# One load of a fused transformer block, its DRAM side written as eight groups of sixteen rows

## Chip, cores, metric

The kernel runs on one core of a Trainium2 chip. The metric is device time in microseconds of one execution. Three runs of the kernel before gave 1547.07 to 1547.58, median 1547.14.

## What is computed

The reference is one transformer block on 256 tokens of width 2048: a gated spatial unit and a forgetting attention side by side, then a mixture of 32 experts in four groups. Only the experts matter here; a token goes to two of them.

```python
def expert_block(args):
    xi, e = args
    return (jax.nn.silu(xi @ w_g[e]) * (xi @ w_u[e])) @ w_d[e]

yb = lax.map(expert_block, (xb, blk_e)).reshape(P, D)
y = jnp.zeros((T + 1, D), jnp.float32).at[buf_tok].add(yb.astype(jnp.float32) * buf_gate[:, None])[:T]
```

`w_g` and `w_u` are 2048 x 512 for each expert, `w_d` ("down") is 512 x 2048, all float32: 12 MB an expert, and every expert's weights are read.

## The kernel before

The first part (projections, attention, output projection, router) takes some 640 us. Then a loop goes over the 32 experts. For each, `gather` collects its tokens (up to 32), `hidden` multiplies them by gate and up, `times_up` combines the two, and `down` multiplies by the down matrix.

The weights come through SBUF homes of 16 KB a partition (`hT0`, `hT1`, `so0`, `so1`, `rb`, two ring tiles, `third`, and `ex` with `bm` as two halves). Each expert has six chunks `t = 6 e + ...` of 2 MB: two of gate, two of up, two of down. `order` lists the chunks, `free` the homes that are empty, and `load` pairs the next chunk with the next home and issues its DMA from SP. `used_up` gives a home back after PE has read it and calls `load` again. So SP's queue holds one stream of weight loads, and each of them waits for its home and for an earlier landing.

The last two experts (30 and 31) are treated apart. Their down matrices are cut into column blocks, listed in `BLOCKS`: four of 512 columns for expert 30; three of 512 and two of 256 for expert 31. A block of n columns is 128 rows (partitions) of 4 n floats, so 8 KB a row for 512 columns, 1 MB in all. `layout` on the host lays these blocks side by side in `we_l`, 32 KB a partition and expert, and `load` fetches each with a DMA of its own (line 568). `block(e, c0, n)` names the place in SBUF. For expert 31 the chunk that holds the columns from 1024 on goes to the home `hT0`: blocks (31, 1024) with 512 columns, (31, 1536) and (31, 1792) with 256 each. These are the last three loads of the program; in the profile they are `hT<-in_we_l`.

Behind the expert loop stands a loop over `todo`, the nine blocks in order. For each, `columns` (line 927) multiplies on PE into `y_ps`; ACT (line 1075) copies the result into `fine` (also under the name `hT` in the profile), and DVE (line 1076) writes the rounding rest beside it. Then, for the block before this one, `add_columns` spreads the rows to the tokens with four matmuls (line 936), and DVE adds them, times the gate, to the accumulator (line 941, `mT` in the profile). PE's order is fixed by `keep`: `y_ps` of block i, then the four matmuls of block i - 1. When a block of expert 31 has been added, SP stores two pieces of 128 tokens (line 1082).

Of the kernel before, what the change touches and what calls it, by code (L numbers as in the profile page):

```python
# [26 lines left out]
NE = NG * EPG  # L27
# [4 lines left out]

BLOCKS = {NE - 2: ((0, 512), (512, 512), (1024, 512), (1536, 512)),
          NE - 1: ((0, 512), (512, 512), (1024, 512), (1536, 256), (1792, 256))}
QW = 2048
HW = 2 * QW
CUTS = (0, 2, 4, 6, 8, 12, 16)
# [8 lines left out]
def hybrid_block(ctx: ExitStack, tc: tile.TileContext, a, out, dbg=None):  # L46
    nc = tc.nc
# [62 lines left out]
    def early(pool, name, dt=F32R):  # L110
        return pool.tile([P, QW], dt, tag=name, name=name)

    home = {}

    def wide_tile(pool, name, dt=F32R):
        t = pool.tile([P, HW], dt, tag=name, name=name)
        home[id(t)] = pool, name
        return t

    def halves(pool, name):  # L120

        both = [wide_tile(pool, f"{name}{k}") for k in range(2)]
        return [[t[:, i * QW:(i + 1) * QW].rearrange("p (a b) -> p a b", a=8) for i in range(2)] for t in both]

# [426 lines left out]
    def load(n=1):  # L551


        while n and free and order:
            n -= 1
            t = order.popleft()
            slot[t] = free.popleft()
            w = slot[t][0]
            e, m, c = t // 6, t // 2 % 3, t % 2
            src = a[names[m]][e * P:(e + 1) * P]  # L560
            if m < 2 or e not in BLOCKS:
                n0 = HW // len(w)
                for i, wi in enumerate(w):
                    nc.sync.dma_start(wi, src[:, c * HW + i * n0:c * HW + (i + 1) * n0])
            else:
                for c0, n0 in BLOCKS[e]:
                    if c0 // 1024 == c:
                        nc.sync.dma_start(block(e, c0, n0), a["we_l"][e - NE + 2][:, 4 * c0:4 * (c0 + n0)])

    def quarter(t, c):  # L570

        w = slot[t][0]
        return w[c] if len(w) == 2 else w[0][:, c * QW:(c + 1) * QW]

    def block(e, c0, n0):

        o = c0 % 512
        return quarter(6 * e + 4 + c0 // 1024, c0 // 512 % 2)[:, 4 * o:4 * (o + n0)]

    def room(tiles, keep=True):  # L580

        for t in tiles:
            free.append((t if isinstance(t, tuple) else (t,), keep))

    def used_up(t):

        if slot[t][1]:
            free.append(slot[t])
            load()

    mT = None
    for n in range(4):
# [18 lines left out]
        if n == 3:  # L611
            room([wide_tile(ra, nm, F32) for nm in ("hT0", "hT1")])
            load(AHEADS[0])
# [3 lines left out]
        if n == 3:  # L617
            room([wide_tile(ra, "so0", F32)])
            load(AHEADS[1])
# [67 lines left out]
    lent = wide_tile(mp, "mT0", F32)  # L687
    y, acc0 = lent[:, :QW], lent[:, QW:]
    room([lent], False)
# [28 lines left out]
    lent = wide_tile(mp, "mT1", F32)  # L718
    acc = [acc0, lent[:, QW:]]
    room([lent], False)  # L720
# [348 lines left out]
    for i in range(len(todo) + 1):  # L1069
        nxt = None  # L1070
        if i < len(todo):
            e, c0, n = todo[i]
# [4 lines left out]
        if i:  # L1077
            e, c0, n = todo[i - 1]
# [8 lines left out]
def layout(inputs):  # L1087
    import numpy as np

    g = {k: np.asarray(v) for k, v in inputs.items()}  # L1090
    c = np.ascontiguousarray

    def ktile(w):

        return w.reshape(-1, P, w.shape[1]).transpose(1, 0, 2)

    def chunks(w):
        return [ktile(w[:, i:i + 512]) for i in range(0, w.shape[1], 512)]

    def rows4(w):  # L1100

        return c(w.reshape(NE, 4, P, 4 * DE).transpose(0, 2, 1, 3).reshape(NE * P, 16 * DE))

    def columns(e, i, n):

        return g["w_expert_down"][0][e].reshape(4, P, D)[:, :, i:i + n].transpose(1, 0, 2).reshape(P, 4 * n)

    x = g["x"][0]
    w = g["w_in"][0]
    order = [w[:, SW:2 * SW], w[:, 0:SW], w[:, 2 * SW:5 * SW]]  # L1110
    g0 = 5 * SW + NH
    for n in range(4):
        order += [w[:, g0 + n * 512:g0 + (n + 1) * 512], w[:, g0 + D + n * 512:g0 + D + (n + 1) * 512]]
    wp = np.concatenate([g["w_proj_sgu"][0], g["w_proj_fox"][0]], axis=0)
    return {
        "x": c(x.reshape(NT, P, D).transpose(1, 0, 2)),
        "xT": c(ktile(c(x.T))),
        "g1T": c(g["norm1_g"][0].reshape(KT, P).T),
        "g2T": c(g["norm2_g"][0].reshape(KT, P).T),
        "g2p": c(g["norm2_g"][0].reshape(4, P, 4).transpose(1, 2, 0)),  # L1120
        "w_in": c(np.stack([t for o in order for t in chunks(o)])),
        "wf": c(ktile(w[:, 5 * SW:5 * SW + NH])),
        "b_forget": c(g["b_forget"][0]),
        "b_gate": c(g["b_gate"][0]),
        "ln_g": c(g["sgu_ln_g"][0]),
        "ln_b": c(g["sgu_ln_b"][0]),
        "wsT": c(g["w_spatial"][0].transpose(2, 0, 1)),
        "bsT": c(g["b_spatial"][0].T),
        "qkg": c(np.stack([g["q_norm_g"][0], g["k_norm_g"][0]], axis=1)),
        "w_proj": c(np.stack(chunks(wp))),  # L1130
        "w_out": c(np.stack(chunks(g["w_out"][0]))),
        "wr": c(ktile(np.concatenate([g["w_router_group"][0], g["w_router_expert"][0], np.zeros((D, 64 - NG - NE), np.float32)], axis=1))),
        "br": c(np.concatenate([g["b_router_group"][0], g["b_router_expert"][0]])),
        "we_g": rows4(g["w_expert_gate"][0]),
        "we_u": rows4(g["w_expert_up"][0]),
        "we_l": c(np.stack([np.concatenate([columns(e, i, n) for i, n in BLOCKS[e]], axis=1) for e in BLOCKS])),
        "we_d": c(g["w_expert_down"][0].reshape(NE, 4, P, D).transpose(0, 2, 1, 3).reshape(NE * P, 4 * D)),
    }

# [16 lines left out]
```

## Time and profile before

| | us |
|---|---|
| median of three runs | 1547.14 |
| profiled execution | 1547.18 |
| its span, first to last instruction | 1545.3 |
| PE busy in the span | 1315.8 |
| DVE busy | 594.0 |
| ACT busy | 412.0 |
| POOL busy | 30.1 |

PE is the busiest engine by its total, but that is a sum over stages with different limits. [...]

### The profile page before, as it was taken

To read this page: it belongs to the slowest core of one execution; us is meant where nothing else is said; L and a number is where in the kernel's file an instruction comes from. 1 tells how busy PE (TensorE), PEld (TensorE's weight loads), DVE (VectorE), ACT (ScalarE), POOL (GpSimd) and SP (SyncE) were. 2 spreads that over 40 slices of the span, in tenths; PEclk is the share of its full clock that TensorE was granted. 3 is DMA by queue.
4 is the path that set the end of the run, shared out by engine and by line. 5 is a ranking of instruction groups with operands and counts; after the bars stand their busy time and mean duration, and the time that the engine had idled before them with its cause. 6 is when DMAs were issued, how large, how long until landed. Compare 5 with 4: busy or idle time off the path is not lost. (4 is left out here: it accounts for less than half of the span.)

```text
span 1545.3 us, 18445 instructions
## 1 busy us (share of the span) xinstructions
PE 1315.8 (85%) x7480; PEld 744.7 (48%) x7480; DVE 594.0 (38%) x1139; ACT 412.0 (27%) x755; POOL 30.1 (2%) x37
## 2 busy tenths in 40 slices
PE   9999999999999999898766768767767867867777
PEld 8788888888888878433222222212212212222222
DVE  6766766665665655422112212112112212112124
ACT  6645455545555444111100110010010100100001
POOL 0300100000000000000000000000000000000000
PEclk9999999999999999999888989879888889888899
DMA  9554453454546865899999999999999999999998
GB/s 384 229 213 170 164 209 145 151 211 183 219 177 249 350 245 191 349 427 426 427 426 426 425 429 426 427 426 427 426 426 427 426 427 427 426 427 427 426 427 328
DMA packets 48743, 523.53 MB, mean 339 GB/s; under 512 B 5904, under 2 KB 10640, under 8 KB 14480
## 3 DMA queue, kind: packets, MB, share of 16 engines
q1 hardware_dynamic: 47360, 520.22, 81.5%
q10 hardware_dynamic: 1296, 2.11, 0.5%
q8 instruction: 60, 0.98, 0.3%
q14 instruction: 27, 0.22, 0.0%
HBM read 520.21 MB, written 2.10 MB: 338 GB/s over the span
## 5 line engine op out<-in xcount | busy, mean ns | idle before, releaser
L240 DVE TENSOR_TENSOR wl<-w,wh 128x512 fp32r<-128x512 f32 x220 | 151.0, 690 | 110.1 <-ACT wh L239 109.7
L239 ACT ACTIVATE wh<-w 128x512 fp32r<-128x512 f32 x220 | 138.0, 631 | 151.3 <-PE z L247 74.3
L245 PE MATMUL z<-wh,hT 128*128 128x512 f32 x382 | 151.5, 397 | 0.4 <-ACT wh L239 0.4
L246 PE MATMUL z<-wl,hT 128*128 128x512 f32 x382 | 149.4, 391 | 2.5 <-DVE wl L240 2.5
L247 PE MATMUL z<-wh,hT 128*128 128x512 f32 x382 | 149.1, 390 | 0.0
L884 ACT ACTIVATE q<-ps 128x256 f32<-128x256 f32 x64 | 24.5, 383 | 457.8 <-PE ps L876 436.5
L885 DVE COPY q<-ps 128x256 f32<-128x256 f32 x64 | 27.1, 424 | 266.3 <-ACT q L884 266.3
L920 DVE COPY mT<-y_ps 32x512 f32<-32x512 f32 x60 | 41.1, 684 | 196.5 <-PE y_ps L911 176.9
L887 PEld LDWEIGHTS s_ps<-four,q 128*128 128x128 f32 x512 | 65.3, 196 | 98.4 <-ACT q L884 95.9
L918 ACT ACTIVATE mT<-y_ps 32x512 f32<-32x512 f32 x60 | 35.3, 588 | 284.8 <-DVE mT L920 284.8
L887 PE MATMUL s_ps<-four,q 128*128 128x32 f32 x512 | 72.8, 286 | 33.0 <-ACT q L884 33.0
L876 PE MATMUL ps<-hT,xT 128*32 128x512 f32 x512 | 83.5, 741 | 20.0 <-DMA hT<-in_we_g_dram 13.3
L876 PE MATMUL ps<-w,xT 128*32 128x512 f32 x480 | 74.6, 690 | 16.7 <-DMA w<-in_we_g_dram 11.2
L876 PE MATMUL ps<-so,xT 128*32 128x512 f32 x384 | 69.2, 807 | 20.5 <-DMA so<-in_we_g_dram 20.4
L829 PE MATMUL x_ps<-x,sel 128*32 128x512 f32 x512 | 85.0, 655 | 0.7 <-DVE sel L825 0.7
L246 PEld LDWEIGHTS z<-wl,hT 128*128 128x128 f32 x382 | 71.8, 188 | 18.7 <-DVE wl L240 4.6
L245 PEld LDWEIGHTS z<-wh,hT 128*128 128x128 f32 x382 | 71.7, 188 | 15.5 <-issue 0.8
L247 PEld LDWEIGHTS z<-wh,hT 128*128 128x128 f32 x382 | 71.7, 188 | 15.0
L245 PE MATMUL z<-ex,hT 128*128 128x512 f32 x194 | 76.1, 393 | 0.0
L246 PE MATMUL z<-ex,hT 128*128 128x512 f32 x194 | 75.6, 390 | 0.0
L247 PE MATMUL z<-ex,hT 128*128 128x512 f32 x194 | 75.6, 390 | 0.0
L240 DVE TENSOR_TENSOR wl<-third,wh 128x512 fp32r<-128x512 f32 x75 | 59.4, 802 | 34.1 <-ACT wh L239 34.1
(304 smaller groups left out, 1840.6 us busy)
## 6 DMA issues: line engine op xcount, KB each, us to landing
w<-in_w_in_dram SPq DMA_DIRECT2D x20, 2048.0 KB, 7.3
hT<-in_we_u_dram SPq DMA_DIRECT2D x20, 2048.0 KB, 34.3
w<-in_we_u_dram SPq DMA_DIRECT2D x19, 2048.0 KB, 34.3
so<-in_we_d_dram SPq DMA_DIRECT2D x18, 2048.0 KB, 34.3
third<-in_w_in_dram SPq DMA_DIRECT2D x14, 2048.0 KB, 7.3
hT<-in_we_g_dram SPq DMA_DIRECT2D x12, 2048.0 KB, 34.3
so<-in_we_u_dram SPq DMA_DIRECT2D x12, 2048.0 KB, 36.7
so<-in_we_g_dram SPq DMA_DIRECT2D x12, 2048.0 KB, 34.3
```

The source lines that it names most:

```text
L239: nc.scalar.activation(wh, wv, AF.Copy)
L240: nc.vector.tensor_tensor(wl, wv, wh.bitcast(F32), ALU.subtract)
L245: nc.tensor.matmul(z[tb], hi, wh[:, i - j], start=first, stop=False)
L246: nc.tensor.matmul(z[tb], hi, wl[:, i - j], start=False, stop=False)
L247: nc.tensor.matmul(z[tb], lo, wh[:, i - j], start=False, stop=final)
L829: nc.tensor.matmul(x_ps[32 * c:32 * c + 32], sel[:, tb], x1[:, tb, c * 512:(c + 1) * 512], start=(tb == 0), stop=(tb == NT - 1))
L876: nc.tensor.matmul(ps[32 * i:32 * i + 32], xT[:, i, c], w[:, i], start=(c == 0), stop=(c == 3))
L884: nc.scalar.activation(q[:, 0:256], ps[:, 0:256], AF.Copy)
L885: nc.vector.tensor_copy(q[:, 256:], ps[:, 256:])
L887: nc.tensor.matmul(o[:, j * CAP:(j + 1) * CAP], q[:, j * P:(j + 1) * P], four, start=True, stop=True)
L918: nc.scalar.activation(o, i, AF.Copy)
L920: nc.vector.tensor_copy(o, i)
```

## The change

One load out of the nine of line 568, that of block (31, 1024), takes its data from another DRAM tensor, `we_8`. The host fills `we_8` with the same 128 rows of 2048 floats, as eight groups of sixteen rows and one row of zeros behind each group. The load reads the sixteen rows of each group. Its destination in SBUF is the same 128 partitions, in the same order. As built, the source is described by 8 groups x 16 rows x 2048 floats instead of 128 rows x 2048 floats, and the destination as 128 x 1 x 2048 instead of 128 x 2048. No instruction moves on any engine and no wait differs.

```diff
+EIGHTS = ((NE - 1, 1024),)
...
                 for c0, n0 in BLOCKS[e]:
                     if c0 // 1024 == c:
-                        nc.sync.dma_start(block(e, c0, n0), a["we_l"][e - NE + 2][:, 4 * c0:4 * (c0 + n0)])
+                        o, i = block(e, c0, n0), a["we_l"][e - NE + 2][:, 4 * c0:4 * (c0 + n0)]
+                        if (e, c0) in EIGHTS:
+                            i = a["we_8"][:, 0:16]
+                        nc.sync.dma_start(o, i)
...
         "we_l": c(np.stack([np.concatenate([columns(e, i, n) for i, n in BLOCKS[e]], axis=1) for e in BLOCKS])),
+        "we_8": c(np.concatenate([columns(*EIGHTS[0], 512).reshape(8, 16, 2048), np.zeros((8, 1, 2048), np.float32)], axis=1)),
```

## Rows read from the trace of the kernel before

**Rows 1.** The page: span, and the DMA share and rate in forty slices.

```profile
span 1545.3 us, 18445 instructions
...
DMA  9554453454546865899999999999999999999998
GB/s 384 229 213 170 164 209 145 151 211 183 219 177 249 350 245 191 349 427 426 427 426 426 425 429 426 427 426 427 426 426 427 426 427 427 426 427 427 426 427 328
```

**Rows 2.** Chain of waits, its end: start us, us, what.

```profile
1514.12 19.80 DMA hT<-in_we_l_dram
1533.92 0.14 issue
1534.05 1.07 PE y_ps L927 x8
1535.12 0.67 PE ps L936 x2
```

**Rows 3.** Timeline, PE and DVE: start, us, instruction, idle time before it and releaser.

```profile
1531.57 1.06 PE L927 MATMUL y_ps<-rb,h 128*32 128x512 f32 x8 [0.28 <-DMA rb<-in_we_l_dram]
...
1532.56 1.20 PE L936 MATMUL ps<-hT,gt 128*128 128x512 f32 x4
...
1534.05 1.07 PE L927 MATMUL y_ps<-hT,h 128*32 128x512 f32 x8 [0.29 <-DMA hT<-in_we_l_dram]
...
1535.05 1.20 PE L936 MATMUL ps<-hT,gt 128*128 128x512 f32 x4
...
1535.82 0.75 DVE L941 SCALAR_TENSOR_TENSOR mT<-ps,gw,mT 128x512 f32<-128x512 f32 x1 [0.48 <-PE ps L936]
...
1536.18 0.64 PE L927 MATMUL y_ps<-hT,h 128*32 128x256 f32 x8
...
1538.54 0.64 PE L927 MATMUL y_ps<-hT,h 128*32 128x256 f32 x8
```

**Rows 4.** Instructions by tile, rb (two loads), then hT (three): issues, time to landing.

```profile
L568 SPq DMA_DIRECT2D rb<-in_we_l_dram x2: 328/328/328, 1506.9 to 1511.6; - x2
...
DMA to landing us min/median/max: 19.8/20.9/22.1
...
L568 SPq DMA_DIRECT2D hT<-in_we_l_dram x3: 327/327/328, 1514.1 to 1519.1; - x3
...
DMA to landing us min/median/max: 17.4/18.6/19.8
```

**Rows 5.** Table by stretch: us, busy by engine (instructions), clock, DMA share, GB/s.

```profile
1520.00:1524.00 4.00, 2.43 (x16) 0.86 (x12) 1.28 (x2) 1.20 (x2) 0.00 (x0) 1.00 1.02 426
...
1527.00:1528.00 1.00, 1.00 (x10) 0.34 (x3) 0.91 (x2) 0.26 (x1) 0.00 (x0) 1.00 1.01 418
1528.00:1529.00 1.00, 0.82 (x4) 0.34 (x2) 0.61 (x1) 0.34 (x1) 0.00 (x0) 1.00 0.68 279
...
1530.00:1531.00 1.00, 1.00 (x8) 0.67 (x4) 0.53 (x2) 0.60 (x1) 0.00 (x0) 1.00 0.57 238
1531.00:1532.00 1.00, 0.72 (x7) 0.19 (x8) 1.00 (x2) 0.00 (x0) 0.00 (x0) 1.00 0.55 229
1532.00:1533.00 1.00, 1.00 (x10) 0.37 (x3) 0.87 (x2) 0.31 (x1) 0.00 (x0) 1.00 0.51 209
1533.00:1534.00 1.00, 0.76 (x4) 0.30 (x2) 0.67 (x2) 0.28 (x1) 0.00 (x0) 1.00 0.50 201
```

**Rows 6.** The page, DMA queues: packets, MB, share of sixteen engines' span.

```profile
q8 instruction: 60, 0.98, 0.3%
```

**Rows 7.** Waits of SP's queue, 1500 to 1546: us in total, times, longest.

```profile
SPq L568 <- DMA w<-in_we_l_dram: 2.1, 1, 2.1
```

**Rows 8.** Table by stretch, PE alone: us, busy (matmuls), clock, DMA share, GB/s.

```profile
1504.00:1508.00 4.00, 1.18 (x12) 1.00 1.00 420
...
1510.00:1512.00 2.00, 0.73 (x8) 0.95 1.00 418
1512.00:1514.00 2.00, 2.00 (x12) 0.50 1.02 426
```

**Rows 9.** Timeline of PE, two gaps: start, us, instruction, idle time before it.

```profile
1511.61 3.51 PE L876 MATMUL ps<-third,xT 128*32 128x512 f32 x16 [1.27 <-DMA third<-in_we_u_dram]
...
1521.64 1.06 PE L927 MATMUL y_ps<-w,h 128*32 128x512 f32 x8 [1.41 <-DMA w<-in_we_l_dram]
```

## The prediction

> **What bounds the kernel now.** I read the page first: from the eighteenth of the forty slices on, the DMA row stands at 9 and the GB/s row at 425 to 429 in all but the last, so the expert phase runs at the pace of the weight stream [rows 1]. The change touches the last microseconds, so the chain of waits, read from its end, comes next. It leaves the DMA queue at 1533.92, when the load `hT<-in_we_l` issued at 1514.12 has landed after 19.80 us; 0.14 us later PE starts `y_ps` L927, and from there it is work of PE, ACT and DVE to the end [rows 2]. That load is the one that the change rewrites: block (31, 1024).
>
> The timeline shows the rhythm that it stands in. PE runs the blocks of 512 columns at 1531.57 and 1534.05, and each start has 0.28 or 0.29 us of idle time before it, ended by a DMA [rows 3]. The landings agree: the two `rb` blocks, issued at 1506.9 and 1511.6, took 22.1 and 19.8 us and landed at 1529.0 and 1531.4; the block in question landed at 1533.92 and the last load, issued at 1519.1, at 1536.5 after 17.4 us [rows 2, 4]. A block of 1 MB thus lands 2.49 us after the one before (1533.92 - 1531.43). The two blocks of 256 columns behind it start at 1536.18 and 1538.54 [rows 3], when their data (the last at 1536.5) are there: the changed block is the last that PE waits for.
>
> One thing does not show on the page: the sixteen DMA engines are not level. If they were, all would be busy until 1536.5. Instead the DMA share falls from 1.01 in 1527 to 1528 to 0.68 (eleven of sixteen), 0.57 and, in 1532 to 1534, 0.51 and 0.50 (eight of sixteen) [rows 5]. Five engines have finished all loads by about 1528, some 8 us before the last; the eighth of the leading half leaves at about 1532.5, 4 us before it; eight engines lag. GB/s falls with the share (426 at 1.02, 209 at 0.51), so an engine's own rate, 426/1.02/16 = 26.1 GB/s in full traffic and 209/0.51/16 = 25.6 with half of them, hardly depends on how many others run. A candidate for the lag is the instruction queue q8: 60 packets at 0.3% of sixteen engines' span [rows 6], by estimate 0.003 x 16 x 1545 = 74 us of engine time, or 9 us each if always the same eight engines serve it. No row names an engine.
>
> **The change part by part.** On every engine's queue the instructions keep their places; one of SP's loads has another source. Packets, bytes and destination stay: 128 rows of 8 KB.
>
> *Issue.* The nine loads of that line take 0.33 us of SP each; the next issue waits 2.1 us for an earlier landing in any case [rows 4, 7]. A dearer issue is hidden up to these 2.1 us, and the load has 19.80 us from issue to landing. Beyond that it would hold up the two last loads, which have about 1.0 us (1536.18 against a landing midway between 1533.92 and 1536.5) and 2.0 us to spare. Value zero.
>
> *Address pattern on the DRAM side.* Rows that lie 8 KB apart replace rows 32 KB apart. No row prices that; an engine at 26.1 GB/s shows no stall that it could lose. Value zero, ends a few tenths either way.
>
> *The split over engines.* This term decides. Before, 128 rows over sixteen engines are eight packets each, 2.49 us, or 0.311 us a packet. Eight groups cannot be dealt evenly over sixteen engines without cutting a group. If each group goes to one engine, eight engines carry sixteen packets each: 16 x 0.311 = 4.98 us, and the other eight go straight on to the two last loads. [...]
>
> What that does to the end depends on which eight. (a) If a lagging engine is among the carriers, it starts where it does now and needs 2.49 us more: landing 1533.92 + 2.49 = 1536.41, PE at 1536.54 instead of 1534.05. The two last loads move by at most as much, to about 1537.7 and 1539.0, and PE wants them at 1538.67 and 1541.03: still in time. ACT and DVE work on what PE delivers (DVE waited 0.48 us for `ps` at 1535.82 [rows 3]), so nothing absorbs it: end +2.49. (b) If the carriers are exactly the leading eight, the slowest of them, 4 us ahead of the last, has finished the block before at about 1527.4 and this one at 1532.4. PE is then free at 1532.56 + 1.20 = 1533.76 and, as in the unblocked start at 1536.18 (0.07 before the end of a `ps` run that began at 1535.05), starts at 1533.69: end -0.36, all that the wait holds. (c) If the leading eight carry it but their packets take longer than 0.311 us, because eight engines write rows that sixteen wrote before and the lagging ones are still writing to all the others: at double time the slowest lands at 1527.4 + 9.95 = 1537.4, end +3.5; the middle between (b) and that is +1.6, and above double it is more.
>
> [...]
>
> **How it adds up.** The profiled execution took 1547.18 us for a span of 1545.3, 0.04 above the median of 1547.14. Likeliest is a landing later by about one pitch: (a) in full, and (c) lies around it. The rows give no reason why the eight carriers should be just the eight leaders, and one laggard among them is enough. 1547.18 + 2.49 - 0.04 = 1549.6.
>
> **The rivals.**
> *It balances the engines, (b).* For it: the lag is real, and exactly one half of the engines lags [rows 5], as a fixed half of them would. Against it: half a chance at best that it is the right half, and the packets must keep 0.311 us. 1547.14 - 0.36 = 1546.8. More cannot come out, since PE's wait for this block is only that long.
> *Slower by far: lagging carriers that also get in each other's way.* Place: the writes into `hT`. At double packet time the block lands 9.95 us after 1531.43, at 1541.38 instead of 1533.92: +7.5, 1554.6. It decides from the point where a packet of the carriers takes 0.35 us (16 x 0.35 = 5.6, that is +3.1). Against it: rates per engine do not fall anywhere in the stream [rows 5]. [...]
> *The longer gap costs PE's clock.* [...] In (a) PE idles 2.8 us (1533.76 to 1536.54). If the clock falls there, the next pieces of the chain, 1.07 + 0.67 us, double: +2.49 + 1.74, 1551.4. Against it: PE is busy 0.72 to 1.00 of each microsecond just before [rows 5], and the gap of 1.41 us at 1521.64 left the clock at 1.00 [rows 5, 9].
> *The change does nothing.* If the rows are dealt over sixteen engines as before, all stays: 1547.1. For it: both sides still hold 128 rows of 8 KB.
>
> **How the numbers follow.** Forecast (landing later by about 2.5 us) 0.45; balance 0.21; colliding lagging carriers 0.15; clock 0.08; nothing 0.11. What a measurement of this kernel can tell from no change is about 0.2%, 3.1 us. Forecast, balance and nothing lie within it, 0.77, of which I take off 0.03 for the upper part of (c) and 0.01 for more gain than the wait shows: same 0.73, slower 0.26, faster 0.01. The range runs from the balance case, less 0.2 for scatter (1546.6), over the clock case to 1552.0; left out are the collisions, 0.15, and a little of the rest.
>
> **What would show it.** (a): `y_ps<-hT` starts near 1536.5, with a DMA wait of about 2.8 us before it, everything behind moved alike; the DMA share stays at 0.5 to about 1539. (b): that row starts near 1533.7 with no DMA wait, and the share no longer has its step at 0.50 before the outputs. (c) and the collision: the landing lies later than the carriers' sixteen packets explain. Nothing: landings 2.49 us apart as before. I am wrong altogether if another load than this one ends the last wait, if the issue takes microseconds, or if the end moves without this landing.

## The result, and the profile after

The changed kernel takes 1557.45 us (median of four runs, 1555.81 to 1558.51) against 1547.31 before: ratio 1.0063, 95% interval 1.0051 to 1.0076. It is slower by 10.1 us, four times what I had forecast and outside my range. The profiled execution took 1558.51 for a span of 1556.7, so 11.33 us more than the profiled one before.

Its chain of waits near the end (start us, us, what) answers to [rows 2]:

```profile
1513.76 29.52 DMA hT<-in_we_dram
1543.28 0.14 issue
1543.41 1.94 PE y_ps L932 x8
1545.35 2.00 PE ps L941 x4
```

The right load ends the last wait, but it lands at 1543.28 instead of 1533.92, 9.36 us later. The PE pieces behind it take longer too: `y_ps` 1.94 instead of 1.07, and the four `ps` matmuls 2.00, to be set against the 1.20 of four in [rows 3] (the 0.67 of [rows 2] counts two of them). The timeline of PE (start, us, instruction, idle time before it and its releaser) answers to [rows 3]:

```profile
1523.91 1.07 PE L932 MATMUL y_ps<-w,h 128*32 128x512 f32 x8 [0.43 <-DMA w<-in_we_l_dram]
...
1528.54 1.79 PE L932 MATMUL y_ps<-w,h 128*32 128x512 f32 x8 [2.44 <-DMA w<-in_we_l_dram]
...
1533.15 1.06 PE L932 MATMUL y_ps<-rb,h 128*32 128x512 f32 x8 [0.83 <-DMA rb<-in_we_l_dram]
...
1537.76 1.07 PE L932 MATMUL y_ps<-rb,h 128*32 128x512 f32 x8 [2.41 <-DMA rb<-in_we_l_dram]
...
1543.41 1.94 PE L932 MATMUL y_ps<-hT,h 128*32 128x512 f32 x8 [2.76 <-DMA hT<-in_we_dram]
```

This is the main surprise: the loads *ahead* of the changed one are late too. The second `rb` block, an unchanged load issued at 1511.3, starts PE at 1537.76 instead of 1531.57. The loss has begun before the changed block is wanted.

The table by stretch (us, busy by engine with instructions, TensorE's granted clock as a share of full speed, DMA share, GB/s) answers to [rows 5]:

```profile
1520.00:1524.00 4.00, 2.27 (x16) 0.97 (x20) 1.63 (x3) 1.15 (x2) 0.00 (x0) 1.00 1.04 389
1524.00:1526.00 2.00, 2.00 (x12) 0.74 (x11) 1.39 (x3) 0.60 (x1) 0.00 (x0) 1.00 1.04 233
1526.00:1527.00 1.00, 0.10 (x1) 0.00 (x0) 1.00 (x3) 0.00 (x0) 0.00 (x0) 1.00 0.96 197
...
1530.00:1531.00 1.00, 1.00 (x6) 0.65 (x3) 0.00 (x0) 0.60 (x1) 0.00 (x0) 0.50 0.95 221
1531.00:1532.00 1.00, 1.00 (x4) 0.52 (x2) 0.48 (x1) 0.00 (x0) 0.00 (x0) 0.50 0.81 168
...
1535.00:1536.00 1.00, 0.35 (x2) 0.00 (x0) 1.00 (x2) 0.00 (x0) 0.00 (x0) 1.00 0.96 217
1536.00:1537.00 1.00, 0.00 (x0) 0.00 (x0) 0.93 (x2) 0.00 (x0) 0.00 (x0) 1.00 0.62 123
...
1538.00:1539.00 1.00, 1.00 (x9) 0.24 (x2) 0.00 (x0) 0.12 (x1) 0.00 (x0) 0.99 0.39 123
1539.00:1540.00 1.00, 1.00 (x3) 0.73 (x3) 0.16 (x1) 0.48 (x1) 0.00 (x0) 0.50 0.29 90
1540.00:1541.00 1.00, 0.65 (x2) 0.00 (x0) 1.00 (x2) 0.00 (x0) 0.00 (x0) 0.50 0.15 61
```

From about 1523.5 to 1536 nearly all of the sixteen engines are busy (share 0.80 to 1.04), yet together they move only 168 to 233 GB/s. In 1526 to 1527 one engine's rate is 197/0.96/16 = 12.8 GB/s, half of the 26.1 worked out from [rows 5]. At 1540 a share of 0.15, about two engines, is all that is left, and PE waits for it.

The page has no row by packet. I read them out of the trace: median time of one 8 KB packet, by the microsecond in which it starts, and the times at which the engines finish their share of block (31, 1024), read from its semaphore.

```
8 KB packet, median us    1520  1522  1524  1526  1528  1530  1532  1534  1537  1540  1542
  kernel after            0.31  0.31  0.63  0.64  0.62  0.58  0.51  0.53  0.32  0.31  0.31

shares of block (31, 1024) landed at
  before   1525.86 .91 1526.07 .08 .10 1527.22 1528.67 1529.97 | 1532.15 .25 .31 .41 .44 1533.59 .66 .92
  after    (8 at once on issue)  1532.50 .84 1533.09 1534.96 1537.67 1538.65 | 1543.25 .28
```

(The bar stands between the engines that finish early and those that finish late.) So eight engines carry the load, where sixteen did before. No row names an engine, but the times tell them apart: six of the carriers are of the leading half and two, which finish 4.6 us behind the last of those, of the lagging half. For 13 us an 8 KB packet takes 0.51 to 0.64 us at the median instead of 0.31, on carriers and others alike.

### The profile page after: what moved, and what is told of

Its sections match the earlier page's. It is cut to its first block, busy times and chain, and to the rows that moved or that the text cites. A ratio compares the mean times of both kernels' runs of the same rounds, so it can differ in the third digit from the quotient of the medians.

```text
span 1556.7 us, 18445 instructions
## 1 busy us (share of the span) xinstructions
PE 1327.2 (85%) x7480; PEld 748.7 (48%) x7480; DVE 594.3 (38%) x1139; ACT 412.0 (26%) x755; POOL 30.1 (2%) x37
```

## Experiments

**The DRAM side.** The same block from a tensor of its own, in 128 rows without groups (here and in the next runs the host lays out `we_8` to match; the diffs show the load alone):

```diff
-                            i = a["we_8"][:, 0:16]
+                            i = a["we_8"]
```

> The block comes from its own DRAM tensor with its 128 rows of 8 KB one behind another, described as 128 rows: the new place in DRAM without the groups. If the loss comes from the groups (which engines carry it, and where each of them writes), the time is that of before, 1547.3 within 0.5. If it comes from reading rows 8 KB apart in DRAM, most of the 10 us loss stays: 1554 to 1558.

1547.25 against 1546.89, ratio 1.0001 (0.9992 to 1.0011). Another place in DRAM and another distance between rows cost nothing; the loss sits in the grouping.

**Sixteen groups of eight rows.**

```diff
-                            i = a["we_8"][:, 0:16]
+                            i = a["we_8"][:, 0:8]
```

> Sixteen groups of eight rows in place of eight of sixteen. If an engine serves whole groups, all sixteen engines carry eight packets each again, but each writes eight neighbouring partitions. Theory halving (eight engines with twice the packets are the loss): time of before, 1547.3 within 0.5. Theory collision (engines that write neighbouring partitions get into the way of others): packets of twice 0.311 us while the block is under way, 1549 to 1554. Theory DRAM side: 1552 to 1558.

1553.07, ratio 1.0043 (1.0026 to 1.0060). Here all sixteen engines carry eight packets each, as before, and still 6 us are lost. Its timeline of PE:

```profile
1533.28 1.93 PE L932 MATMUL y_ps<-rb,h 128*32 128x512 f32 x8 [1.40 <-DMA rb<-in_we_l_dram]
...
1540.08 1.07 PE L932 MATMUL y_ps<-hT,h 128*32 128x512 f32 x8 [0.73 <-DMA hT<-in_we_dram]
```

Half as many engines is therefore not the larger part of the loss.

**Four loads of 32 partitions, each of eight groups of four rows.**

```diff
-                            i = a["we_8"][:, 0:16]
-                        nc.sync.dma_start(o, i)
+                            for j in range(4):
+                                nc.sync.dma_start(o[32 * j:32 * j + 32], a["we_8"][j][:, 0:4])
+                        else:
+                            nc.sync.dma_start(o, i)
```

> The block as four loads of 32 partitions, each as eight groups of four rows: still eight engines with sixteen packets each, but four neighbouring partitions of every 32 to an engine instead of sixteen in a row. Theory halving: about one block time over before, 1549.6 to 1550. Theory collision: fewer meetings, packets near 0.31 us for half of the block: 1548 to 1551. Theory DRAM side: as the change, 1554 to 1558.

1554.07, ratio 1.0046 (1.0030 to 1.0063). Eight engines again, each with four rows of its own in every 32 partitions. Packets took about twice their 0.31 us all the same from 1526.5 to 1536. (The two last loads are issued some 8 us later here, but PE does not wait for them.) At this point my picture, carriers that meet each other, was incomplete: they seemed to meet the other engines too.

**Patterns in the first part.** Eight of the 2 MB loads of the ring of the projections are described in other ways.

> The kernel before; in its front part, where the DMA engines idle most of the time, eight loads of 2 MB (128 rows of 16 KB, 0.613 us a packet) are described in other ways, each nearly alone in flight: eight groups (twice, and once with nine rows of zeros behind each group), sixteen groups, thirty-two groups, plain rows, and four loads of 32 partitions as eight groups or as plain rows. Plain rows: 8 packets an engine, 4.9 us of transfer. Theory halving alone: eight groups 9.8 us at 0.613 us a packet, sixteen 4.9, four times eight 9.8. Theory collision: eight groups 10 to 20 us with packets up to 1.2 us, sixteen 5 to 10 us with packets up to 1.2 us, four times eight groups 9.8 us at 0.613, four times plain rows 10 us at 1.2. Theory DRAM side: the wide spacing differs from the narrow one. Time of the whole: within 10 us of before.

Most plain loads of this ring land 7.0 to 7.6 us after issue in the kernel before; eight groups, nearly alone, took 23.0 us (235.32 to 258.34), and packets of 16 KB 1.15 us at the median instead of 0.61. Of the four aligned loads the last three landed 2.45 and 2.49 us apart (212.32, 214.77, 217.26), four packets of 0.61 an engine: not slowed. The other patterns overlapped with neighbours and settle nothing. The whole took 1562.0 us in its one run, 15 above the kernel before, where I had expected at most 10.

**PE kept busy.** Dummy matmuls ahead of the late blocks:

```diff
+FILL = {(NE - 2, 1536): 26, (NE - 1, 0): 9, (NE - 1, 512): 24, (NE - 1, 1024): 28}
...
+            keep_warm(FILL.get((e, c0), 0))
```

> The changed kernel with 87 dummy matmuls on PE (128 columns each, results unused) placed ahead of the column blocks at which PE waits longest: 26 before (30,1536), 9 before (31,0), 24 before (31,512), 28 before (31,1024). They are meant to fill the idle time, not to lengthen it. Theory: of the 10.1 us of loss, 9.4 is the late landing of the block and about 1.9 is the granted clock of 0.50 in the tail behind it (9.02 us from the first y_ps<-hT to the last addition, against 7.09 before), the rest scatter. If so, the landings stay where the changed kernel has them and the tail takes about 7.1 us: about 1555.5. Rival: the tail is long for another reason (the two last loads, the outputs): clock near 1.00 in the records, tail still 9 us, 1557.4. A third way: the dummies run at the low clock themselves and push y_ps back: later than 1557.5.

The landing is where it was, and the tail is short. The last addition of DVE starts at 1541.14 before, 1552.43 after and, in this kernel, 1550.37, each time the last `mT` row of the timeline. In this order:

```profile
1541.14 0.88 DVE L941 SCALAR_TENSOR_TENSOR mT<-ps,gw,mT 128x256 f32<-128x256 f32 x2 [0.27 <-PE ps L936]
```

```profile
1552.43 0.88 DVE L946 SCALAR_TENSOR_TENSOR mT<-ps,gw,mT 128x256 f32<-128x256 f32 x2 [0.27 <-PE ps L941]
```

```profile
1543.29 1.06 PE L933 MATMUL y_ps<-hT,h 128*32 128x512 f32 x8 [2.13 <-DMA hT<-in_we_dram]
...
1550.37 0.88 DVE L947 SCALAR_TENSOR_TENSOR mT<-ps,gw,mT 128x256 f32<-128x256 f32 x2 [0.27 <-PE ps L942]
```

From `y_ps` to there it is 7.08 us, against 9.02 after (1543.41 to 1552.43) and 7.09 before (1534.05 to 1541.14). The table by stretch shows the granted clock, of after and then of this kernel:

```profile
1543.00:1547.00 4.00, 3.58 (x12) 1.39 (x12) 0.46 (x1) 0.60 (x1) 0.00 (x0) 0.50 0.21 79
```

```profile
1543.00:1547.00 4.00, 3.67 (x22) 1.36 (x22) 1.95 (x4) 0.98 (x2) 0.00 (x0) 1.00 0.19 68
```

In the profiled executions the clock explains 1.9 us. In the medians it does not show: 1557.00 (1556.45 to 1557.52) against 1557.45, with ranges that overlap. The profiled executions are the shortest of the four here and the longest of the four there, so their difference is the largest that these runs give. How often the clock falls in the runs that were not profiled stays open.

**The same load, written aside.** Source, place in the queue and 128 rows of 8 KB are kept, but the destination lies in DRAM; block (31, 1024) is multiplied from what `hT0` holds.

```diff
-                            i = a["we_8"][:, 0:16]
-                        nc.sync.dma_start(o, i)
+                            o, i = a["aside"][:, 0], a["we_8"][:, 0:16]
+                        d = nc.sync.dma_start(o, i)
+                        if e == NE - 1:
+                            keep(d)
```

> The changed kernel, in which the eight-group load has the same source, the same place in SP's queue and 128 rows of 8 KB as destination, but these lie in DRAM; block (31, 1024) is multiplied from whatever hT0 holds, so PE does not wait for this load. Theory (the engines meet where they write into neighbouring partitions): without writes into SBUF the packets of all loads stay at about 0.31 us, the rb blocks land at their old times (1528.97 and 1531.43 in the kernel before), and the time is that of the kernel before or up to 2 us under it, 1545 to 1547.5. Rival 1 (eight engines with sixteen packets each, or the source, slow the others whatever is written): packets near 0.6 us from about 1523 on as in the changed kernel, rb blocks at 1533 and 1537.6, time 1553 or more. Rival 2 (writes into DRAM cost more than writes into SBUF): the eight engines' packets alone are longer, the others keep 0.31 us; the two last loads come late by that, 1548 to 1553.

1547.63 against 1547.37, ratio 1.0000 (0.9991 to 1.0010). Its timeline of PE and its table by stretch:

```profile
1528.94 1.06 PE L934 MATMUL y_ps<-rb,h 128*32 128x512 f32 x8 [0.29 <-DMA rb<-in_we_l_dram]
...
1531.43 1.07 PE L934 MATMUL y_ps<-rb,h 128*32 128x512 f32 x8 [0.29 <-DMA rb<-in_we_l_dram]
...
1537.54 0.64 PE L934 MATMUL y_ps<-hT,h 128*32 128x256 f32 x8 [1.56 <-DMA hT<-in_we_l_dram]
```

```profile
1524.00:1526.00 2.00, 2.00 (x12) 0.82 (x12) 1.53 (x4) 0.60 (x1) 0.00 (x0) 1.00 0.96 401
```

The time alone would not tell, because PE no longer waits for this load. The rows do: the `rb` blocks start PE as in the kernel before, and the engines keep their rate, 401/0.96/16 = 26.1 GB/s. Here eight engines read the same groups and slow nobody; the slow packets of the changed kernel need this load's writes into SBUF. This run gives more. Its eight shares landed by themselves at 1527.94, .99, 1528.05, 1529.56, 1531.50, 1532.11 and, on the two lagging carriers, 1536.14 and 1536.33. That is what sixteen packets on eight engines cost where nobody is slowed: 1536.33 - 1533.92 = 2.41 us.

**Each pattern alone.** Behind the last outputs of the kernel before, loads of 1 MB into the place of the block, one after another:

```diff
+    for _ in range(2):
+        probe(first, "rows", 0)
+        probe(first, "eight", 16)
+        probe(first, "sixteen", 8)
+        probe(first, "thirtytwo", 4)
+        probe(first, "four", 32)
+        probe(first, "foureight", 4, 4)
...
+    probe(first, "eight", 16)
+    probe(second, "rows", 0)
...
```

> The kernel before, with loads of 1 MB into the place of block (31, 1024) added behind the last outputs, each waiting for the one before, so that each is alone in flight: 128 plain rows; eight groups of sixteen rows; sixteen of eight; thirty-two of four; four of thirty-two; four loads of thirty-two partitions with eight groups of four rows each; all of it twice, and at the end the eight groups together with 128 plain rows into the other half of the home, and the four loads likewise. At 0.311 us for a row of 8 KB and some 2.4 us from issue to the first data, plain rows should take 2.49 us of packets. Theory of shared writes (engines that write into the same stretch of partitions halve each other): eight groups 9.95 us of packets (16 each at 0.62), thirty-two groups and sixteen groups near 4.98, four groups 19.9, the four loads of aligned groups 4.98 or less, since their engines do not meet. Rival (eight engines and no more): eight groups 4.98, sixteen and thirty-two 2.49, four 9.95. Together with a plain load: by the theory that load's packets go to 0.6 to 0.9 us while both run; by the rival it lands 2.5 to 5 us after issue plus latency.

From the trace, second round (issue to last landing, median of the 128 packets):

```
                       landed after   packet      engines
128 rows                    4.67        0.31        16
8 groups of 16             11.55        0.58         8
16 groups of 8              7.44        0.61        16
32 groups of 4              5.38        0.31        16
4 groups of 32             17.05        0.35         4
4 loads of 8 groups of 4    8.23        0.31         8
8 groups and, at once, a plain load elsewhere:
  plain load's shares after 8.4 to 8.7 on the eight engines without groups
```

Eight and sixteen groups slow themselves, thirty-two do not. For thirty-two I had expected 0.62 us a packet; four groups lie between, with some packets at 0.31 and some at 0.55 and over. A plain load beside the eight groups needs 8.4 us and more instead of 4.7 on engines that carry nothing of the groups.

**Which partitions meet.** Groups of chosen lengths alone, then four aligned loads (eight groups of four rows into the same 32 partitions, on eight engines) beside a plain load of 16 KB rows. Parts of the diff:

```diff
+        for g, n in PAIRS:
+            keep(nc.sync.dma_start(first[0:g * n], a["g%d_%d" % (g, n)][:, 0:n]))
...
+    for lo in (0, 64, 32, 96):
+        for o in (hT0, so):
+            for h in range(2):
+                keep(nc.sync.dma_start(o[lo:lo + 32, h * QW:(h + 1) * QW], a["g8_4"][:, 0:4]))
+        keep(nc.sync.dma_start(more, a["wide"]))
```

> The kernel before, with loads added behind its end that show which engines get in each other's way. First, one at a time in an otherwise quiet queue: g groups of n rows of 8 KB into the first g x n partitions of hT0, for (2,16), (2,32), (2,64), (4,8), (4,16), (8,4), (8,8), (8,16), all of it twice. Then four times five loads at once: four aligned ones (eight groups of four rows into the same 32 partitions, from partition 0, 64, 32 and 96 on in turn) and a plain one of 128 rows of 16 KB into another home. [...] Rival 1: any group of rows is slower than plain rows once two or more engines take part: all pairs near 0.6. Rival 2: two loads in flight at once slow each other wherever they write: all four places alike. [...]

```
alone, us per 8 KB packet: median (three quarters at most), second round
(2,16) 0.31 (0.31)   (2,64) 0.31 (0.31)   (4,8) 0.31 (0.33)    (8,4) 0.31 (0.58)
(2,32) 0.39 (0.61)   (4,16) 0.48 (0.61)   (8,8) 0.56 (0.62)    (8,16) first round 0.61 (0.64)

beside a plain load: its 16 KB packets while groups are in flight, and its landing
on the eight engines without groups, after issue
from partition 0    median 0.72   8.1 to 8.4
from partition 32   median 0.61   8.2 to 8.5
from partition 64   median 1.18   9.7 to 9.8
from partition 96   median 1.20   9.5 to 9.7
```

The first packet of each engine takes up to 1 us, which weighs in the short rows: (8,4) has four packets an engine, and behind the first they take 0.31. Two groups on partitions 0 to 15 and 16 to 31, or 0 to 63 and 64 to 127, do not slow each other (0.31). Two on 0 to 31 and 32 to 63 do, for part of their packets (median 0.39, three quarters at most 0.61; (2,32) drifts out of step). The second table fits the riddle of the four loads: the same groups leave a plain load nearly alone at 0 and 32 (0.72 and 0.61 us) and double its packets at 64 and 96 (1.18 and 1.20). That would be so if the eight engines that carry no groups write partitions 64 to 127 of a plain load, and the eight carriers intrude there; this is my inference from the two tables. In the changed kernel group 0 has partitions 0 to 15 and group 2 has 32 to 47, and the upper four groups lie from 64 on: by the same inference, with each group on one engine, carriers meet each other, and they meet the eight engines that carry no group. Why just these ranges meet, and 0 to 15 with 16 to 31 do not, no row shows.

**Thirty-two groups in the kernel.**

```diff
-                            i = a["we_8"][:, 0:16]
+                            i = a["we_8"][:, 0:4]
```

> The changed kernel with the same block described by thirty-two groups of four rows (and a row of zeros behind each) instead of eight of sixteen. Alone in flight this pattern's packets took 0.31 us, where eight of sixteen took 0.56 and sixteen of eight 0.60. Theory (what counts is which engine writes which partitions; groups of four rows are dealt out as plain rows are): time of the kernel before, 1547.4, within 0.2%, landings 2.49 us apart. Rival (any description in groups disturbs the stream, with its dearer issue and its other addresses): near the sixteen groups' 1553.

1547.25 against 1547.42, ratio 1.0000 (0.9990 to 1.0009). The block's shares landed from 1525.91 to 1533.85 on sixteen engines, within 0.1 us of before. Its row of PE, to be read beside [rows 3]:

```profile
1534.09 1.06 PE L932 MATMUL y_ps<-hT,h 128*32 128x512 f32 x8
```

Groups as such are harmless here, and so are their source and their dearer issue (0.65 us for this load, 0.33 before). What is left as the cause is which engine writes which partitions. No row names an engine, so that dealing is inferred from the numbers of shares and from the pairs above.

**Two blocks in eight groups.**

```diff
-EIGHTS = ((NE - 1, 1024),)
+EIGHTS = ((NE - 1, 512), (NE - 1, 1024))
...
-                            i = a["we_8"][:, 0:16]
+                            i = a["we_8"][EIGHTS.index((e, c0))][:, 0:16]
```

> The changed kernel with two blocks, (31, 512) and (31, 1024), described by eight groups of sixteen rows. If the loss is packets at double length wherever carriers and others write at once, the stretch of slow packets grows by the 2.5 to 5 us that another block of 16 packets a carrier takes: 1560 to 1564. If the loss of the one block was a single disturbance of the stream: 1557.5. If the two blocks follow one another on the same eight engines and the others are done early: the second block's 16 packets run at 0.31 behind them, +5: 1562.

1560.70 (1559.11 to 1564.74), ratio 1.0081 (1.0064 to 1.0097). Slow packets now stretch from 1521.5 to 1541.5. That is 20 us instead of 13; I had expected 2.5 to 5 more. The median is 3.3 us above one block, so the loss does grow with the dose. The profiled execution is the longest of the four, 1564.74. In it the second block's packets were slow too until 1541.5 and ran at 0.31 on the two lagging carriers behind that, so that between the first and third expectation the run can't choose.

**Why the engines are not level.** 34 small matmuls more on PE, each with a weight load, so 68 instructions, for each of the experts 0 to 29 in the kernel before (my expectation calls all 68 matmuls):

```diff
+        if e not in BLOCKS:
+            ps = trm.tile([P, 512], F32, tag="tr", name="ps")[:, :16]
+            for _ in range(34):
+                keep(nc.tensor.matmul(ps, onesb, onesb[:, :16], start=True, stop=True))
```

> The kernel before with 68 small matmuls (16 columns, results unused) more on PE for each of the experts 0 to 29, 2040 in all, where PE has time to spare; the loads are the same. Reason for it: the engines are not level at the end, eight are some 8 us behind, and the instruction queue's 60 packets of 16 KB are my candidate. Theory: PE's instructions are fetched by eight of the sixteen engines, so 2040 more of them at some 270 a packet (2040 x 64 bytes / 16 KB = 8 packets of about 1.05 us, or somewhat more) set the laggards back by one round of about 1 to 1.6 us: 1548 to 1549, and more packets in q8. Rival: the lag comes from something else, and the time stays at 1547.3 within 0.5 us with the packets of q8 up all the same.

1549.11 against 1547.37, ratio 1.0014 (1.0005 to 1.0024). The page's row for the instruction queue, to be read beside [rows 6]:

```profile
q8 instruction: 68, 1.11, 0.3%
```

Eight packets more for 2040 instructions, so about 64 bytes each (8 x 16,384 / 2040). Block (31, 1024) was finished by the first engine at 1525.66 (before 1525.86) and by the last at 1535.16 (1533.92): the leaders stay, the laggards fall back by 1.24 us. Fetching PE's instructions does make eight engines lag. At 1.24 us for a round of eight, the 36 of the 60 packets that fall into the expert phase would give 5.6 of the 8.1 us. The trace of the kernel before, read load by load, shows the rest. A load's later eight shares come this long after its first:

```
load landed at   packets so far   the later eight shares, us after the first
1209.5                 48         4.6  4.7  4.8  4.9  4.9  5.0  5.0  5.1
1240.0                 49         4.7  4.8  4.9  4.9  4.9  5.0  5.1  6.2
1318.8                 52         4.9  4.9  5.0  5.0  6.2  6.3  6.3  6.5
1424.3                 56         6.2  6.3  6.3  6.4  6.4  6.5  6.6  6.6
```

Each packet sets one engine back, by some 1.5 us against the first, and eight packets set back all of the later eight. At 603 us all shares came within 0.7 us. From the 25th packet (645 us) to the 56th are four rounds, which make the 6.3 us, and the next three packets put three engines at 7.7 to 8.1. The spread of some 4 us within the leading half has another cause, which stays open.

## Why the prediction was wrong

**Right.** The bound and the load: the weight stream sets the pace, and this load ends PE's last wait. The issue costs 0.80 us instead of 0.33, and it is hidden. The address pattern costs nothing (ratio 1.0001 without the groups). Eight engines carry sixteen packets each (eight shares, 128 packets), a lagging engine is among them, and that alone costs 2.41 us by the load written aside, against my 2.49. Case (a) was the right mechanism for that part, and the lagging half lags for the reason that I had named. (Its 60 packets took 62 us of engine time in all, 7.8 us an engine, where I had worked out 74 and 9 from a rounded share.)

**Wrong: the size of a packet.** The step that failed is "The split over engines", where I kept 0.311 us for case (a) and put double packets into a rival with 0.15. The evidence held against that rival was "rates per engine do not fall anywhere in the stream". That row could not decide: its loads are all plain rows, whose packets stayed at 0.31 us. That each engine keeps to partitions of its own there, so that no two meet, is my inference: pairs that met took 0.39 us and more at the median. The row says nothing on a load that is dealt otherwise. The double time of case (c) and of that rival was an assumption that no run had shown. What the runs showed in its place: 0.51 to 0.64 us a packet from 1523 to 1536, for all loads in flight.

**Wrong: who pays.** Even the rival, nearest with 1554.6 to the measured 1557.45, counted doubled packets for the carriers alone and started from an unchanged 1531.43 of the load ahead. But the six leading carriers begin the block while the lagging engines still write the blocks ahead of it. These slow down too: the second `rb` block landed at 1537.62 instead of 1531.43, 6.2 us late, before the last carriers had started on theirs. From there the block took 5.66 us, about the 4.98 of case (a).

**Wrong: one case or the other.** The clock stood as a rival beside the forecast, at +1.74 if it falls to the 0.50 of [rows 8]. It comes on top of the late landing: 1.93 us in the profiled execution. The clock had fallen before PE waited for the changed block: it was 1.00 in 1536 to 1537 and 0.50 from 1539 on, behind the idle 2.41 us that the late `rb` block had left at 1537.76. My 1.74 took `y_ps` and two of the four `ps` matmuls at double time; what the runs showed in its place, at 0.50, is 1.94 for 1.07 and, for the four, 2.00 for 1.20.

The sum for the profiled executions: 2.41 for sixteen packets on eight engines (1536.33 - 1533.92), 6.95 for slow packets (1543.28 - 1536.33), 1.93 for the clock (9.02 - 7.09), together 11.29 of 11.33. The first two terms go by one profile each, the third falls out of a pair; their split is good to some tenths.

## What to carry to other kernels

When a transfer's shape changes, ask first how it will be dealt out: how many engines, and which partitions each writes compared with the transfers beside it. Here one load dealt otherwise made every transfer in flight pay, the ones ahead included (168 to 233 GB/s instead of 426), so price such a pattern at the whole stream's rate. And an even rate in the old profile, 26.1 GB/s an engine here, is no evidence that nothing can collide: it may be even because everything is dealt alike.

## What the runs showed of the hardware

- One engine with 8 KB packets moves 26.1 GB/s (0.31 us a packet). Two groups on partitions 0 to 31 and 32 to 63 had a median of 0.39 and three quarters at most 0.61; on 0 to 15 and 16 to 31, or 0 to 63 and 64 to 127, both kept 0.31.
- One load of 1 MB in eight groups brought sixteen engines from 426 to about 210 GB/s for some 13 us.
- Thirty-two groups of four rows behaved like plain rows (0.31 us, landing within 0.1 us), sixteen groups of eight did not (0.61 us, 6 us lost), although both ran on sixteen engines.
- The sixteen engines were up to 8 us apart after 0.9 ms of steady loads: each instruction packet of 16 KB set one of the later eight back by some 1.5 us against the first. Eight packets more made the last share land 1.24 us later.
